# A hybrid decoder layer on one core: the split of the mixed values in four steps, and when the forgetting heads' decay rows are loaded

## Chip, core and metric

One core of one Trainium2 chip runs the whole layer in one launch. The metric is the device time of that launch in microseconds (us). Everything is float32; TensorE multiplies in a format called fp32r here, so the kernel makes a product of two or three passes over parts of its operands: the rounded value (hi) and what the rounding left (lo).

## What is computed

A layer of 1024 positions and 1024 channels: one input projection feeds eight heads with a sliding window (A) and eight forgetting heads (B), their outputs side by side go through one output projection, and an MLP follows. Of the reference:

```python
xn = rmsnorm(x, attn_norm_g)
proj = jnp.einsum('bsd,de->bse', xn, w_in)
qa, ka, va, qb, kb, vb, f_logit = jnp.split(proj, IN_SPLITS, axis=-1)
...
out_a = swa_sinks_attention(qa, ka, va, sink_logits)      # 8 heads of 64, window 128
...
log_f = jax.nn.log_sigmoid(f_logit + b_forget)
out_b = forgetting_attention(qb, kb, vb, log_f)           # 8 heads of 64, causal
mixed = jnp.concatenate([out_a, out_b], axis=-1)
x = x + jnp.einsum('bse,ed->bsd', mixed, w_out)
hn = rmsnorm(x, mlp_norm_g)
hid = jnp.square(jax.nn.relu(jnp.einsum('bsd,df->bsf', hn, w_up)))
x = x + jnp.einsum('bsf,fd->bsd', hid, w_down)
```

In a forgetting head the score of query t and key s gets c[t] - c[s] added, where c is the running sum of log f; the term c[t] falls out of the softmax, so what is left is one row of 1024 numbers a head, the **decay row**.

## The kernel before

**Stages.** The projection of the A heads and of the first pair of B heads comes first, then the A heads in two groups of eight units (`heads_a`), then the B heads in four pairs p = 0 to 3, of eight units each (`heads_b`): units 0 to 3 are the first head of the pair (h = 0), 4 to 7 the second (h = 1). A unit is 256 queries of one head, in the order `ORDER_B`. The MLP follows; it uses Strassen's scheme of seven products.

**A unit.** `scores_b` (L590) makes the score products `spb` for 128 queries and up to 512 keys at a time; VectorE adds the decay row `cb` and finds the extreme in one instruction (L607, printed as ISA), ScalarE takes the exponential. `mix_b` (L631) transposes the probabilities (`tpb`), evicts them into hi (`pth`, ScalarE, L347) and lo (`ptl`, VectorE, L348), multiplies with the values (`pvb`), joins the two accumulated parts (`mtb`, L660) and stores the result to `mix_d` in DRAM (L663; `mta`, L511, for the A heads). Scores run `DEPTH` = 2 units ahead of the mixing.

**Fillers.** Between the units stand projection products `ps` for the next pair of B heads and, in the last pair, products `po` of the output projection (`out_first`). `PACE` gives the number of units of scores behind which each is placed, and `tc.issue_after(x)` keeps an instruction behind x in the order. Their weights come as rows `wr` (L205), each into a buffer that has to be free, and are split into `wh` (cast, ScalarE) and `wl` (subtraction, POOL).

**What sets the order.** A scheduler orders each engine's instructions by modelled times and priorities; `prep` and the two offsets `HPO` and `HPA` raise the priority of what they enclose. Each engine then runs its list in order and waits where an operand or a buffer is missing. All transfers are issued by SyncE, in order too: one that waits holds up all that stand behind it.

**The mixed values.** The probabilities are not divided by their sum before the products, except in the last pair of B heads. So the 14 halves (seven pairs of heads e, two halves c of 512 positions) go back from DRAM to be divided and split, in `split_mix(e)` (L532): `mixr` is the half of `mix_d`, `mixn` the inverse sums from `rd_d`, spread over the partitions in two transfers (L538, L540); VectorE multiplies them (L541); ScalarE casts (hi) and POOL subtracts (lo); the result `mixs` is stored (L543) and loaded later as the tiles `mix0` to `mix6` for the output projection (L758). There is one buffer each of `mixr`, `mixn` and `mixs`. `SPLITS` names the unit (p, u) in which `split_mix(e)` is called; both halves are written there at once, and where they come to stand is the scheduler's choice.

**The decay rows.** `prep_k(p, h)` (L575) also loads the row `cb` of that head (L578, 512 KB, spread over 128 partitions) into one of two buffers. `ahead` calls it for h = 0 in unit 5 and for h = 1 in unit 7 of the pair before.

Of the kernel before, what the change touches and what calls it, by code (L numbers as in the profile page):

```python
# [8 lines left out]
F32 = mybir.dt.float32  # L9
# [37 lines left out]
SPLITS = ((0, 4), (0, 7), (1, 1), (1, 4), (1, 6), (2, 5), (3, 5))  # L47
# [4 lines left out]
def hybrid_layer(  # L52
# [435 lines left out]
    def mix_a(pts, g, i):  # L488
# [21 lines left out]
        for j in range(2):  # L510
            nc.sync.dma_start(mix_d[2 * g + j, :, i * P : (i + 1) * P], mt[:, j, :])  # L511
# [20 lines left out]
    def split_mix(e):  # L532

        for c in range(2):
            cs = slice(c * 512, (c + 1) * 512)
            m, q = (ap2.tile([P, 512], F32, tag=n, name=n, bufs=1) for n in ("mixr", "mixn"))
            hl = ap2.tile([P, 2, 512], F32R, tag="mixs", name="mixs", bufs=1)
            nc.sync.dma_start(m, mix_d[e][:, cs])  # L538
            for h in range(2):
                nc.sync.dma_start(q[rows_of[h], :], rd_d[2 * e + h, cs].partition_broadcast(HD))  # L540
            nc.vector.tensor_tensor(out=m, in0=m, in1=q, op=ALU.mult)  # L541
            split(hl[:, 0], hl[:, 1], m, nc.scalar, nc.gpsimd)
            nc.sync.dma_start(  # L543
                mixs_d[e][:, :, cs].rearrange("c p s -> p c s"), hl.bitcast(F32)
            )
# [29 lines left out]
    def prep_k(p, h):  # L575
        heads[p, "k1", h] = make_k_b(qkb[p], P, p, h)
        cb = ap2.tile([P, S], F32, tag="bias", name=f"cb{p}{h}", bufs=2)
        nc.sync.dma_start(cb, c_d[2 * p + h].partition_broadcast(P))  # L578
        heads[p, "cb", h] = cb
# [5 lines left out]
    def scores_b(p, qp, h):  # L585
        q1, k1, k2, cb = heads[p, "q"][h], heads[p, "k1", h], k2_of[h], heads[p, "cb", h]
        probs = []
        for i in (2 * qp, 2 * qp + 1):
# [8 lines left out]
            for c in range((nk + 511) // 512):  # L597
# [9 lines left out]
                nc.vector.tensor_tensor_reduce(  # L607
# [20 lines left out]
        marks.append(pe.ins)  # L628
        return probs

    def mix_b(probs, p, qp, h):  # L631
# [30 lines left out]
        if p < 3:  # L662
            nc.sync.dma_start(mix_d[4 + p, r, ms], mt[r, :])  # L663
        else:
            split(mh[7][r, ms], ml[7][r, ms], mt[r, :], nc.scalar, nc.vector)
# [46 lines left out]

    def heads_b(p):
        for u in range(8):
            qp, h = (ORDER_END if p == 3 and u > 3 else ORDER_B)[u % 4], u // 4
            unit(lambda: scores_b(p, qp, h), lambda got, qp=qp, h=h: mix_b(got, p, qp, h))
            if u == DEPTH:
                prep(prep_v, p, 1)
                if p:
                    prep(inverse_to, 6 + 2 * p, dn_b[(p - 1) % 2], 2)  # L720
                else:
                    prep(inverse_a)
            if (p, u) in SPLITS:
                split_mix(SPLITS.index((p, u)))
# [193 lines left out]
    def up(j):  # L918
# [3 lines left out]
        s = slot(("m5", "m4")[j % 2], "wus", [4, 4, P])  # L922
# [180 lines left out]
    def h_add(c, dt, cs):  # L1103

        nset[1] += 1
        h = slot(("m3", "m5")[nset[1] % 2], "hy", [4, 512])
# [117 lines left out]
```

## Time and profile before

| | us |
|---|---|
| device time, median of 3 runs | 1147.91 (1147.52 to 1148.44) |
| the profiled execution's own time | 1146.44 |
| its span, from the first to the last instruction | 1144.2 |
| TensorE matmul, busy | 1108.6 |
| VectorE, busy | 771.0 |
| ScalarE, busy | 576.4 |
| GpSimd, busy | 381.6 |

The mean granted clock of TensorE was 0.991. PE is TensorE's matmuls, PEld its weight loads, DVE VectorE, ACT ScalarE, POOL GpSimd, SP or SPq SyncE and its queue; L12 is line 12 of the kernel. In a row of the timeline stand the start, the duration, the engine, the line, the operation with its tiles, and in brackets how long the engine had been idle and what released it. In the busy times by stretch stand the bounds, the length, then PE, PEld, DVE, ACT and POOL with their counts of instructions, the granted clock, the share of the DMA engines and GB/s. In the groups of instructions stand the busy time and the mean ns of one, then the idle time of the engine just before them, with what ended it. The chain of work that ended last is followed back from the last instruction, at each step to what released it; "issue" is time in which the engine waited for nothing that the profile shows. In the list of waits of SyncE's queue, the engine and line after the arrow are what was waited for, then the sum, the count and the longest wait.

### The profile page before, as it was taken

What the parts mean: (1) busy time and instruction counts of PE and PEld (TensorE: products, weight loads), DVE (VectorE), ACT (ScalarE), POOL (GpSimd) and SP (SyncE); (2) the same over time, 40 slices, a digit from 0 to 9 for tenths busy, and PEclk for the clock granted to TensorE, in tenths of its full rate; (3) what the DMA queues carried; (4) which work ended last, traced back from release to release, by engine and by line L of the source; (5) the groups of instructions that cost most, each with busy time, mean ns of one, the idle gap of its engine ahead of it and who ended that gap; (6) DMA issues with size and microseconds to landing.
All of it is one profiled execution on the core that took longest, in us unless ns stands there. A gap on an engine that the chain in (4) does not pass through costs nothing.

```text
span 1144.2 us, 15605 instructions
## 1 busy us (share of the span) xinstructions
PE 1108.6 (97%) x5556; PEld 944.9 (83%) x5556; DVE 771.0 (67%) x1316; ACT 576.4 (50%) x1013; POOL 381.6 (33%) x340
## 2 busy tenths in 40 slices
PE   9999899899999999998999999999999999999998
PEld 8998799789898887786888887888888888888876
DVE  6437867756567568799767676865575876674493
ACT  5443877666567666554554544435444433333330
POOL 5651143425533645133232322322221221222241
PEclk9999999999999999999999999999999999999999
DMA  8310121244416647364455443434699777665441
GB/s 308 120 34 22 34 84 41 72 150 162 146 47 238 212 165 248 124 237 148 162 194 193 149 183 123 164 138 166 223 391 352 263 282 253 227 235 190 174 140 45
DMA packets 95646, 195.68 MB, mean 171 GB/s; under 512 B 7128, under 2 KB 19016, under 8 KB 95568
## 3 DMA queue, kind: packets, MB, share of 16 engines
q1 hardware_dynamic: 95424, 194.66, 48.5%
q8 instruction: 44, 0.72, 0.3%
q14 instruction: 34, 0.28, 0.1%
q10 hardware_dynamic: 144, 0.02, 0.0%
HBM read 141.61 MB, written 53.04 MB: 170 GB/s over the span
## 4 chain that ended last, share of the span: by engine, by line
PE 83%; DVE 8%; DMA 3%; issue 2%; ACT 2%; POOL 1%; SPq 0%; DVEq 0%; POOLq 0%; ACTq 0%
PE pd L69 26%; PE pu L69 26%; PE ps L69 12%; PE po L69 4%; PE qps L69 3%; PE spb L69 2%; PE pvb L69 2%; PE tpb L643 2%; PE sp L69 1%; PE tpa L495 1%; DVE ptl L348 1%; DMA mixr<-mix_d 1%; PE pv L69 1%; DMA h_d<-h 1%; DVE sb L607 1%
## 5 line engine op out<-in xcount | busy, mean ns | idle before, releaser
L69 PE MATMUL pd<-hx,wx 128*128 128x512 f32 x1344 | 307.1, 391 | 2.4 <-POOL wx L76 2.4
L69 PEld LDWEIGHTS pd<-hx,wx 128*128 128x128 f32 x1344 | 253.2, 189 | 56.2 <-POOL wx L76 2.9
L69 PE MATMUL pu<-bh,wu 128*128 128x512 f32 x896 | 281.4, 395 | 1.3 <-ACT bh L837 1.3
L69 PEld LDWEIGHTS pu<-bh,wu 128*128 128x128 f32 x896 | 168.7, 188 | 41.3 <-ACT bh L837 1.7
L69 PE MATMUL pu<-bl,wu 128*128 128x512 f32 x448 | 176.7, 395 | 1.9 <-DVE bl L76 1.8
L76 POOL TENSOR_TENSOR wx<-wda,wx 128x1024 fp32r<-128x1024 f32 x28 | 84.6, 3023 | 222.2 <-ACT wx L73 222.2
L73 ACT CAST hx<-hr 128x1024 fp32r<-128x1024 f32 x56 | 59.0, 1054 | 181.0 <-PE pd L69 176.1
L76 DVE TENSOR_TENSOR hx<-hr,hx 128x1024 fp32r<-128x1024 f32 x56 | 74.2, 1332 | 77.1 <-ACT hx L73 77.1
L69 PE MATMUL ps<-wh,xh 128*128 128x384 f32 (+1 forms) x320 | 111.2, 350 | 3.2 <-DVE q L193 2.5
L69 PE MATMUL ps<-wl,xh 128*128 128x384 f32 (+1 forms) x320 | 110.5, 346 | 0.7 <-POOL wl L76 0.7
L69 PE MATMUL ps<-wh,xl 128*128 128x384 f32 (+1 forms) x320 | 110.8, 347 | 0.0
L69 PEld LDWEIGHTS pu<-bl,wu 128*128 128x128 f32 x448 | 84.4, 188 | 22.6 <-DVE bl L76 2.2
L69 PE MATMUL po<-mix,wos 128*128 128x512 f32 x384 | 94.8, 396 | 1.4 <-ACT mix L73 0.8
L76 POOL TENSOR_TENSOR wu<-wus,wu 128x512 fp32r<-128x512 f32 x32 | 47.2, 1476 | 133.8 <-ACT wu L73 129.1
L69 PEld LDWEIGHTS po<-mix,wos 128*128 128x128 f32 x384 | 70.5, 188 | 16.4 <-ACT mix L73 1.5
L73 ACT CAST wu<-wus 128x512 fp32r<-128x512 f32 x64 | 39.1, 618 | 82.6 <-PE pu L69 75.9
L76 POOL TENSOR_TENSOR wu<-wur,wu 128x512 fp32r<-128x512 f32 x32 | 44.0, 1377 | 88.9 <-ACT wu L73 88.9
L76 POOL TENSOR_TENSOR wl<-wr,wh 128x384 fp32r<-128x384 f32 (+1 forms) x47 | 50.0, 1075 | 54.4 <-ACT wh L73 42.2
L905 DVE TENSOR_TENSOR ht<-hb 128x512 f32<-128x512 f32 x32 | 21.8, 722 | 67.1 <-ACT hb L960 67.1
L348 DVE TENSOR_TENSOR ptl<-tpb,pth 128x512 fp32r<-128x512 f32 (+1 forms) x80 | 50.0, 633 | 22.1 <-ACT pth L347 21.5
L69 PEld LDWEIGHTS ps<-wh,xh 128*128 128x128 f32 x320 | 61.3, 192 | 4.2 <-issue 2.8
L69 PEld LDWEIGHTS ps<-wl,xh 128*128 128x128 f32 x320 | 61.3, 192 | 1.9 <-POOL wl L76 1.3
(213 smaller groups left out, 2068.4 us busy)
## 6 DMA issues: line engine op xcount, KB each, us to landing
wda<-in_w_d_dram SPq DMA_DIRECT2D x34, 1024.0 KB, 8.5
hr<-hid_d SPq DMA_DIRECT2D x56, 512.0 KB, 6.2
wur<-in_w_u_dram SPq DMA_DIRECT2D x32, 512.0 KB, 3.6
hid_d<-ht SPq DMA_DIRECT2D x16, 1024.0 KB, 4.4
hid_d<-hb SPq DMA_DIRECT2D x16, 768.0 KB, 3.6
mixs_d<-mixs SPq DMA_DIRECT2D x14, 512.0 KB, 3.4
mix<-mixs_d SPq DMA_DIRECT2D x7, 1024.0 KB, 8.9
wr<-in_w_b_dram SPq DMA_DIRECT2D x32, 192.0 KB, 2.6
```

Of the source, the lines that this page charges most:

```text
L69: return nc.tensor.matmul(out, lhsT, rhs, start=start, stop=stop)
L73: hi_eng.copy(hi, src)
L76: lo_eng.tensor_tensor(out=lo, in0=src, in1=hi.bitcast(F32), op=ALU.subtract)
L348: nc.vector.tensor_tensor(out=lo[:, cols], in0=pt[:, cols], in1=hi[:, cols].bitcast(F32), op=ALU.subtract)
L495: nc.tensor.transpose(tp[:, hh * P : (hh + 1) * P], pts[hh // 2][:, hh % 2, c0 : c0 + P], ident)
L607: nc.vector.tensor_tensor_reduce(out=pr[:, c * 512 : c * 512 + n], in0=sp[:, :n], in1=cb[:, c * 512 : c * 512 + n], scale=1.0, scalar=3e38 ...
L643: nc.tensor.transpose(tp[:, c0 : c0 + P], probs[qi][:, kb * P : (kb + 1) * P], ident)
L905: eng.tensor_tensor(out=out, in0=a, in1=b, op=ALU.subtract)
```

## The change

`split_mix` no longer issues anything itself. It returns four steps: load half 0; multiply and split half 0, load half 1; store half 0, multiply and split half 1; store half 1. `heads_b` runs one of them in each unit, the first in the unit that `SPLITS` names, and six of its seven entries are earlier than before by one or two units. All loads and stores of these steps are kept behind the latest store of mixed values (`stored`), and the products behind the latest reduction of scores (`reduced`). `mixs` has two buffers instead of one.

The decay row of a pair's first head is still asked for in `prep_k`, but behind the latest store of mixed values. That of the second head is asked for in unit 1 of its own pair (`load_c`), not in unit 7 of the pair before.

In the MLP two groups of buffers, `wus` for even j and half of `hy`, move from the pool `zl` on the left side of the memory to `zr` on the right side, under the tag `m5`.

```diff
-SPLITS = ((0, 4), (0, 7), (1, 1), (1, 4), (1, 6), (2, 5), (3, 5))
+SPLITS = ((0, 4), (0, 6), (1, 0), (1, 2), (1, 4), (2, 4), (3, 3))
...
+            st = nc.sync.dma_start(mix_d[2 * g + j, :, i * P : (i + 1) * P], mt[:, j, :])
+        stored.append(st.ins)
...
     def split_mix(e):
...
-            hl = ap2.tile([P, 2, 512], F32R, tag="mixs", name="mixs", bufs=1)
-            nc.sync.dma_start(m, mix_d[e][:, cs])
+            behind(m, mix_d[e][:, cs])
             for h in range(2):
-                nc.sync.dma_start(q[rows_of[h], :], rd_d[2 * e + h, cs].partition_broadcast(HD))
-            nc.vector.tensor_tensor(out=m, in0=m, in1=q, op=ALU.mult)
+                behind(q[rows_of[h], :], rd_d[2 * e + h, cs].partition_broadcast(HD))
+
+        def make(c):
+            m, q = got[c]
+            hl = got[c] = ap2.tile([P, 2, 512], F32R, tag="mixs", name="mixs", bufs=2)
+            with tc.issue_after(reduced[-1]):
+                nc.vector.tensor_tensor(out=m, in0=m, in1=q, op=ALU.mult)
             split(hl[:, 0], hl[:, 1], m, nc.scalar, nc.gpsimd)
-            nc.sync.dma_start(
-                mixs_d[e][:, :, cs].rearrange("c p s -> p c s"), hl.bitcast(F32)
-            )
+
+        def store(c):
+            cs = slice(c * 512, (c + 1) * 512)
+            behind(mixs_d[e][:, :, cs].rearrange("c p s -> p c s"), got[c].bitcast(F32))
+
+        return [
+            lambda: load(0),
+            lambda: (make(0), load(1)),
+            lambda: (store(0), make(1)),
+            lambda: store(1),
+        ]
+
+    stored, reduced = [], []
+
+    def behind(out, in_):
+        with tc.issue_after(stored[-1]):
+            nc.sync.dma_start(out, in_)
...
     def prep_k(p, h):
         heads[p, "k1", h] = make_k_b(qkb[p], P, p, h)
-        cb = ap2.tile([P, S], F32, tag="bias", name=f"cb{p}{h}", bufs=2)
-        nc.sync.dma_start(cb, c_d[2 * p + h].partition_broadcast(P))
-        heads[p, "cb", h] = cb
+        if h == 0:
+            load_c(p, 0)
+
+    def load_c(p, h):
+        cb = heads[p, "cb", h] = ap2.tile([P, S], F32, tag="bias", name=f"cb{p}{h}", bufs=2)
+        behind(cb, c_d[2 * p + h].partition_broadcast(P))
...
-                nc.vector.tensor_tensor_reduce(
+                ttr = nc.vector.tensor_tensor_reduce(
...
+        reduced.append(ttr.ins)
...
-            nc.sync.dma_start(mix_d[4 + p, r, ms], mt[r, :])
+            stored.append(nc.sync.dma_start(mix_d[4 + p, r, ms], mt[r, :]).ins)
...
+            if u == 1:
+                load_c(p, 1)
+            for step in [st.pop(0) for st in splitting if st]:
+                step()
             if (p, u) in SPLITS:
-                split_mix(SPLITS.index((p, u)))
+                splitting.append(split_mix(SPLITS.index((p, u))))
+                splitting[-1].pop(0)()
...
-        s = slot(("m5", "m4")[j % 2], "wus", [4, 4, P])
+        s = slot(*(("m4", "wus", [4, 4, P]), ("m5", "wus", [4, 4, P], F32, "zr"))[j % 2 == 0])
...
-        h = slot(("m3", "m5")[nset[1] % 2], "hy", [4, 512])
+        h = slot(*(("m3", "hy", [4, 512]), ("m5", "hy", [4, 512], F32, "zr"))[nset[1] % 2])
```

How the order of the engines changes is shown at three places. The number behind a name counts tiles and differs between the two kernels.

VectorE in the first pair of B heads, from one `mtb` on (mixed values of one unit, first row) over the products of the split (`mixr`) to the next evictions `ptl`; `q1b` are queries of the next pair, `ss` a reduction for their norm. Before:

```order
L660 TENSOR_TENSOR mtb_2754<-pvb_2724,tmpb_2752 64x256
L541 TENSOR_TENSOR mixr_3108<-mixr_3108,mixn_3109 128x512
L275 SCALAR_TENSOR_TENSOR q1b10_2777<-ptq_2788,gqk_72,q1b10_2777 64x512
L275 SCALAR_TENSOR_TENSOR q1b11_2778<-ptq_2788,gqk_72,q1b11_2778 64x512
L348 TENSOR_TENSOR ptl_2856<-tpb_2850,pth_2855 128x512
L235 TENSOR_REDUCE ss_2955<-sq_2953 128x16
L541 TENSOR_TENSOR mixr_3118<-mixr_3118,mixn_3119 128x512
L240 SCALAR_TENSOR_TENSOR ss_2955<-ss_2955,ep2_77 128x16
L348 TENSOR_TENSOR ptl_2869<-tpb_2863,pth_2868 128x512
```

And with the change, from the same `mtb` on:

```order
L689 TENSOR_TENSOR mtb_2754<-pvb_2724,tmpb_2752 64x256
L635 ISA sb_2972,nmb_2973<-spb_2975,cb01_2481 128x512
L635 ISA nmb_2973 128x1
L275 SCALAR_TENSOR_TENSOR q1b11_2763<-ptq_2773,gqk_72,q1b11_2763 64x512
L348 TENSOR_TENSOR ptl_2841<-tpb_2835,pth_2840 128x512
L551 TENSOR_TENSOR mixr_2757<-mixr_2757,mixn_2758 128x512
L235 TENSOR_REDUCE ss_2949<-sq_2947 128x16
L348 TENSOR_TENSOR ptl_2854<-tpb_2848,pth_2853 128x512
```

Of the two products between this `mtb` and the second `ptl` one is left, and it stands behind the first `ptl` and ahead of the reduction; a score reduction (L635) of the second head has come up.

SyncE's queue later in the same pair, where weight rows `wr` of the next projection and pieces of the split are issued, before:

```order
L543 DMA mixs_d_82<-mixs_3347 128x2x512
L538 DMA mixr_3667<-mix_d_81 128x512
L540 DMA mixn_3678<-rd_d_87 64x512 x2
L663 DMA mix_d_81<-mtb_3105 64x256
L205 DMA wr_3461<-in_w_b_dram 128x384
L205 DMA wr_3467<-in_w_b_dram 128x384
L205 DMA wr_3473<-in_w_b_dram 128x384
L543 DMA mixs_d_82<-mixs_3669 128x2x512
L538 DMA mixr_3677<-mix_d_81 128x512
L205 DMA wr_3479<-in_w_b_dram 128x384
```

And with the change:

```order
L570 DMA mixr_3006<-mix_d_81 128x512
L570 DMA mixn_3007<-rd_d_87 64x512
L205 DMA wr_3465<-in_w_b_dram 128x384
L692 DMA mix_d_81<-mtb_3109 64x256
L570 DMA mixs_d_82<-mixs_3002 128x2x512
L570 DMA mixn_3118<-rd_d_87 64x512 x2
L205 DMA wr_3471<-in_w_b_dram 128x384
L570 DMA mixr_3117<-mix_d_81 128x512
L205 DMA wr_3477<-in_w_b_dram 128x384
L205 DMA wr_3483<-in_w_b_dram 128x384
```

The weight row that stood behind a pair of `mixn` loads and a store of mixed values (`wr_3461`, now `wr_3465`) stands ahead of them; the rows behind it stand between and behind the next piece's loads.

VectorE in the third pair of B heads (p = 2), at the first score reductions of its second head, which read the row `cb21`. Before:

```order
L660 TENSOR_TENSOR mtb_4242<-pvb_4186,tmpb_4240 64x256
L607 ISA sb_4462,nmb_4463<-spb_4465,cb21_4055 128x128
L607 ISA nmb_4463 128x1
L348 TENSOR_TENSOR ptl_4384<-tpb_4378,pth_4383 128x512
L348 TENSOR_TENSOR ptl_4397<-tpb_4391,pth_4396 128x512
L607 ISA sb_4471,nmb_4472<-spb_4474,cb21_4055 128x256
```

And with the change; the load of `cb21` is issued right behind the store of the `mtb` in the first row, where before it was issued a pair earlier:

```order
L689 TENSOR_TENSOR mtb_4240<-pvb_4184,tmpb_4238 64x256
L348 TENSOR_TENSOR ptl_4384<-tpb_4378,pth_4383 128x512
L348 TENSOR_TENSOR ptl_4397<-tpb_4391,pth_4396 128x512
L348 TENSOR_TENSOR ptl_4409<-tpb_4404,pth_4408 128x384
L348 TENSOR_TENSOR ptl_4487<-tpb_4481,pth_4486 128x512
L348 TENSOR_TENSOR ptl_4499<-tpb_4494,pth_4498 128x384
L275 SCALAR_TENSOR_TENSOR q1b30_4518<-ptq_4520,gqk_72,q1b30_4518 64x512
L689 TENSOR_TENSOR mtb_4340<-pvb_4323,tmpb_4338 64x256
L275 SCALAR_TENSOR_TENSOR q1b31_4519<-ptq_4520,gqk_72,q1b31_4519 64x512
L635 ISA sb_4462,nmb_4463<-spb_4465,cb21_4243 128x128
```

The first reduction stood right behind that `mtb` and now stands behind five `ptl`, two `q1b` and the next `mtb`; the second head's score products stand later on TensorE accordingly.

More of the change, by code (lines that the diff above doesn't have):

```diff
@@ L510, in mix_a @@
         for j in range(2):
-            nc.sync.dma_start(mix_d[2 * g + j, :, i * P : (i + 1) * P], mt[:, j, :])
+            st = nc.sync.dma_start(mix_d[2 * g + j, :, i * P : (i + 1) * P], mt[:, j, :])
+        stored.append(st.ins)
     def inverse_to(first, dn, n):
@@ L711, in heads_a @@
             fill()
+    splitting = []
     def heads_b(p):
```

7 lines of the change are left out of this document (5 added, 2 removed).

## The prediction

> **What bounds the kernel now.** I read the page first, then the busy times by stretch, then the chain that ended last, then the rows of each engine where TensorE stood still.
>
> ```profile
> span 1144.2 us, 15605 instructions
> PE 1108.6 (97%) x5556; PEld 944.9 (83%) x5556; DVE 771.0 (67%) x1316; ACT 576.4 (50%) x1013; POOL 381.6 (33%) x340
> PE 83%; DVE 8%; DMA 3%; issue 2%; ACT 2%; POOL 1%; SPq 0%; DVEq 0%; POOLq 0%; ACTq 0%
> ```
>
> TensorE is busy for 97% of the span, so an edit outside it can only give back what TensorE loses by waiting. Where that is, the stretches show (length, then PE busy first):
>
> ```profile
> 200.00:229.00 29.00, 26.05 (x146) 21.40 (x145) 21.41 (x54) 19.77 (x44) 12.72 (x14) 0.94 0.26 73
> 241.00:258.00 17.00, 14.52 (x94) 13.57 (x92) 10.60 (x21) 10.41 (x22) 5.03 (x4) 0.97 0.42 133
> 281.00:298.00 17.00, 14.54 (x92) 12.26 (x91) 11.24 (x25) 9.75 (x24) 13.29 (x18) 1.00 0.53 170
> 298.00:352.00 54.00, 53.76 (x358) 50.70 (x357) 31.88 (x80) 33.34 (x72) 14.94 (x24) 1.00 0.21 65
> 352.00:372.00 20.00, 18.46 (x127) 15.41 (x126) 18.05 (x49) 15.72 (x37) 9.39 (x15) 1.00 0.89 338
> 372.00:424.00 52.00, 51.98 (x295) 44.19 (x294) 27.61 (x66) 32.97 (x68) 27.69 (x30) 1.00 0.58 191
> 424.00:456.00 32.00, 30.50 (x187) 25.46 (x186) 27.47 (x70) 22.07 (x49) 18.09 (x25) 1.00 0.66 227
> 528.00:1144.20 616.20, 609.14 (x2640) 497.26 (x2640) 413.56 (x480) 251.23 (x283) 166.68 (x87) 1.00 0.56 201
> ```
>
> From 528 us the MLP runs, which the diff touches only in the place of two buffers. The forgetting heads run from 200 to 456. There TensorE is idle 2.95 in the first stretch, 2.48 in 241:258, 2.46 in 281:298, 0.24, 1.54, 0.02 and 1.50 in the rest. The two 17 us stretches are those in which the mixed values are split; the chain goes through them:
>
> ```profile
> 244.20 4.24 DMA mixr<-mix_d
> 248.56 0.70 DVE mixr L541
> 249.28 0.63 ACT mixs L73
> 249.98 1.30 POOL mixs L76
> 251.30 0.38 SPq L543
> 251.72 4.03 DMA mixr<-mix_d
> 255.94 0.69 DVE mixr L541
> 256.71 0.61 DVE ptl L348
> ```
>
> One piece of the split follows the other through load, product, cast, subtraction and store, some 7.4 us from load to load, and its product stands in VectorE's queue ahead of `ptl`, for which the value products wait.
>
> **First stall, 241:258.** The rows of VectorE, and TensorE's wait behind them:
>
> ```profile
> 246.89 0.42 DVE L660 TENSOR_TENSOR mtb<-pvb,tmpb 64x256 f32<-64x256 f32 x1
> 253.16 1.22 DVE L235 TENSOR_REDUCE ss<-sq 128x16 f32<-128x1024 f32 x1 [0.66 <-POOL sq L230]
> 255.94 0.69 DVE L541 TENSOR_TENSOR mixr<-mixr,mixn 128x512 f32<-128x512 f32 x1 [1.55 <-DMA mixr<-mix_d]
> 256.63 0.68 DVE L348 TENSOR_TENSOR ptl<-tpb,pth 128x512 fp32r<-128x512 f32 x1
> ```
> ```profile
> 257.37 0.58 PE L69 MATMUL pvb<-ptl,vb 128*128 128x256 f32 x1 [2.48 <-DVE ptl L348]
> ```
>
> The product waits 1.55 for its load and takes 0.69, together 2.24 ahead of that `ptl`. The change has one product in this place, and it comes earlier: behind the first `ptl` and ahead of the reduction `ss`. When its load lands I work out from the issue times and these landings:
>
> ```profile
> cb<-c_d SPq DMA_DIRECT2D x8, 512.0 KB, 3.8
> mixr<-mix_d SPq DMA_DIRECT2D x14, 256.0 KB, 4.0
> mixn<-rd_d SPq DMA_DIRECT2D x28, 128.0 KB, 3.0
> ```
>
> `mtb` ends at 247.3. Its store and the load of `mixr` take about 0.5 each to issue, so `mixr` is issued at 247.8 and lands at 251.8, the second `mixn` at about 252. The product ends near 252.7, before POOL's `sq` releases the reduction at 253.16. So the product lies in a wait that is there anyway, and the `ptl` ends 2.2 us earlier. **Term: -2.2** (bounds -2.48, all the idle time, and 0, if the load lands after 254.4 and the product stands ahead of `ss` for as long as now). The load's wait itself does not vanish; it is moved to where something else waits too.
>
> [...]
>
> **Second stall, 281:298.** SyncE's queue, then POOL and ScalarE:
>
> ```profile
> 275.21 0.47 SPq L538 DMA_DIRECT2D mixr<-mix_d  x1
> 281.22 1.09 SPq L540 DMA_DIRECT2D mixn<-rd_d  x2
> 282.42 0.53 SPq L663 DMA_DIRECT2D mix_d<-mtb  x1
> 283.00 1.60 SPq L205 DMA_DIRECT2D wr<-in_w_b_dram  x3
> ```
> ```profile
> 279.64 1.01 POOL L76 TENSOR_TENSOR wl<-wr,wh 128x384 fp32r<-128x384 f32 x1 [4.59 <-ACT wh L73]
> ```
> ```profile
> 286.40 0.51 ACT L73 CAST wh<-wr 128x384 fp32r<-128x384 f32 x1 [3.68 <-DMA wr<-in_w_b_dram]
> ```
>
> The fourth weight row of the last projection needs the buffer that POOL frees at 280.65. It goes out at 283.00, since the `mixn` pair ahead of it waits for the product that frees `mixn`. It reaches ScalarE 3.40 later, and ScalarE, with the `pth` casts behind the weight's, stands for 3.68. In the changed queue this row is ahead of that pair and of the store: it can go out at about 280.7 and arrive at 284.1, 2.3 earlier. ScalarE's wait falls to about 1.4. The later rows do not gain as much: rows six to eight now stand behind a `mixr` load that waits for POOL's subtraction (now 283.00 + 1.28 = 284.28), where rows five and six go out at 283 to 284.6 now. **Term: -2.0** of the 2.46 idle (bounds -2.46 and 0).
>
> **The other pieces.** Nothing is added to the work: the 14 products, 14 `mixr` and 28 `mixn` loads, 14 `mixs` stores and 8 `cb` loads stay, in another order. The second `mixs` buffer gets no credit, since the chain goes from the store's issue to the next load and not to a cast; nor do the two buffers of the MLP that move to the other side, since they are as large and as many as now. The products:
>
> ```profile
> L541 DVE TENSOR_TENSOR mixr<-mixr,mixn 128x512 f32<-128x512 f32 x14 | 11.9, 852 | 12.7 <-DMA mixr<-mix_d 5.4 <-POOL ptl L649 3.5 <-issue 2.6
> ```
>
> VectorE stood 12.7 us ahead of them, and I expect about as much again, since the new order puts most of them two to six VectorE instructions behind the store that their load follows. Six fall into 298:352, where two fall now and TensorE is idle for 0.24 of 54 us: projection products cover them. Cost 0 (up to 1.5 if that cover ends early). The last pair, 424:456, comes out as it is: about the same products ahead of it, 0 (bounds -1.5 and +1).
>
> **The decay rows.** They are what may cost. A second head's row was loaded a pair ahead, and its load blocked SyncE:
>
> ```profile
> SPq L578 <- DVE nmb L607: 18.8, 5, 10.5
> ```
>
> Behind the longest, 10.5 us, stood only stores, so I credit nothing for it. Now each row follows the store of the pair before, about 0.9 of issues later, and lands 3.8 after that (3.6 to 7.4):
>
> ```profile
> DMA to landing us min/median/max: 3.6/3.8/7.4
> ```
>
> That is about 4.7 behind the `mtb` named in the order. What VectorE has to do meanwhile:
>
> ```profile
> L348 DVE TENSOR_TENSOR ptl<-tpb,pth 128x512 fp32r<-128x512 f32 x48 | 32.6, 687 | 16.3 <-ACT pth L347 16.0
> L348 DVE TENSOR_TENSOR ptl<-tpb,pth 128x384 fp32r<-128x384 f32 x32 | 17.6, 551 | 5.9 <-ACT pth L347 5.5
> L660 DVE TENSOR_TENSOR mtb<-pvb,tmpb 64x256 f32<-64x256 f32 x32 | 13.3, 415 | 11.1 <-ACT tmpb L658 10.5
> L275 DVE SCALAR_TENSOR_TENSOR q1b<-ptq,gqk,q1b 64x512 fp32r<-64x512 f32 x12 | 9.0, 749 | 4.4 <-ACT q1b L274 4.2
> ```
>
> Pair 2: three and two `ptl` (2.06 and 1.10), one `mtb` (0.42), two `q1b` (1.50), 5.1 in all: no wait at 3.8, some 3.2 at 7.4. The transfers there run at 338 GB/s (stretch 352:372), so it may well be late. Worse, five groups of score products that TensorE had there move behind the first output products, which wait for their own weights. 13 matmuls at some 0.2 are 2.6 at most; TensorE then has 24 output products to go on with. I take **+0.8** (0 to +3.2). Pair 1: a reduction, an `mtb` and a `ptl`, 1.8 to 1.9 of VectorE work, against 4.7, a wait of 2.8; TensorE has 22 projection products in front, 3.3 at the 0.15 that one took in 298:352: 0 (up to +2.8). Pairs 0 and 3: 2.5 and 3.6 of work, with 24 projection and 13 output products to cover: 0. The very first row, `cb00`, now follows a late store of the window heads, so three score reductions move behind three `ptl` in 200:229, where TensorE has no filler. They cover 128, 256 and 512 columns, an estimated 1.4 together at the 0.69 that a `ptl` of 512 takes. VectorE's idle time there takes up half: **+0.7** (0 to +1.9, with 0.5 of waiting for the row itself).
>
> **Sum.** -2.2 - 2.0 + 0.8 + 0.7 = -2.7 us. The profiled execution took 1146.44 (span 1144.2 and 2.24 around it), 1.47 below the median of the runs shown; it would become 1143.7. I put the difference on the median, 1147.91, and predict **1145.2**. A measurement of this kernel can tell 0.2% from no change, 2.3 us, so this is just faster.
>
> **Rivals.**
> - All three idle times of the split go (2.48 + 2.46 + 1.50 = 6.4) and the rows cost nothing: 1141.5. For it: the chain's own rows. Against: the products still wait for loads of 4.0 us. Chance 0.17.
> - The change doesn't do what it says: with one `mixr` and one `mixn` buffer the second load of a pair still waits for POOL, so pieces go in series as now, weights six to eight are held behind `mixr`, and half of the first term and all of the second are lost: -1.1 + 1.5 = +0.4, 1148.3. For it: the 12.7 us above stay in the order. Against: the fourth row's place in SyncE's queue. Chance 0.28.
> - Slower: VectorE, in order, stands at the first score reduction of a second head until its row lands. From the point at which TensorE's fillers are shorter than that wait, it is exposed: at `cb00`, pair 1 and pair 2 together 1.9 + 2.8 + 3.2 = 7.9, less 4.2: +3.7, 1151.6. For it: the landings of up to 7.4 and the moved score products. Against: TensorE idle for only 0.24 us in 298:352. Chance 0.17.
> - My forecast, 1142.8 to 1147: 0.38.
>
> Two thirds of the forecast (0.25), all of the first rival and 0.05 of the second lie over 0.2% below 1147.91: faster 0.47. Slower: 0.17, and 0.02 of the second rival: 0.19. The rest, 0.34, is no change. The range, 1140.9 to 1150.6, leaves out about half of the first and of the third rival.
>
> **What would show it.** Right: in the changed profile no wait of 2 us before `pvb` where the first product stands; ScalarE's longest wait before `wh` under 2; TensorE idle under 1 in each stretch that answers to 241:258 and 281:298; VectorE's idle before the products still near 10. Wrong: `wh` still waiting 3 us or more; a score reduction that waits over 2 us for `cb` with TensorE idle beside it; TensorE idle over 3 us more around the first output products.

## The result, and the profile after

The changed kernel takes **1160.26 us** (median of 5 runs, 1158.46 to 1162.37), the kernel before 1147.52 in the same comparison (5 runs, 1141.36 to 1148.44). The ratio is **1.0125**, with a 95% interval of 1.0098 to 1.0152: slower by some 14 us, where 1145.2 was predicted and the range ended at 1150.6. From here on "slower by" is this ratio less one, against runs of the kernel before on the same chip.

The page of the changed kernel: its span, the busy times and the shares of the chain that ended last.

```profile
span 1158.0 us, 15593 instructions
PE 1114.4 (96%) x5556; PEld 945.1 (82%) x5556; DVE 774.4 (67%) x1316; ACT 576.8 (50%) x1013; POOL 382.7 (33%) x340
PE 76%; DVE 9%; DMA 7%; issue 3%; ACT 2%; POOL 1%; SPq 1%; DVEq 0%; POOLq 0%; ACTq 0%
```

TensorE's work is the same 5556 products, but the chain now runs through DMA for 7% of the span (3% before) and through TensorE for 76% (83%). The busy times by stretch say where. The stretches are cut at the first score product of the forgetting heads, the first output product and the first product of the MLP; first the kernel before, then the changed one (bounds, length, PE busy, then the other engines, granted clock, DMA share, GB/s).

```profile
0.00:201.40 201.40, 189.14 (x1100) 179.41 (x1101) 127.54 (x338) 119.42 (x301) 83.36 (x89) 0.97 0.29 92
201.40:369.90 168.50, 158.84 (x1016) 143.74 (x1014) 111.26 (x272) 110.10 (x242) 65.53 (x92) 0.98 0.40 135
369.90:512.20 142.30, 138.74 (x752) 115.08 (x752) 104.43 (x213) 86.94 (x174) 59.76 (x69) 1.00 0.58 196
512.20:1144.20 632.00, 621.92 (x2693) 506.63 (x2691) 427.81 (x495) 259.92 (x298) 172.99 (x91) 1.00 0.55 200
```
```profile
0.00:197.40 197.40, 186.89 (x1100) 177.06 (x1101) 128.48 (x338) 119.89 (x302) 83.41 (x89) 0.99 0.27 88
197.40:372.70 175.30, 159.73 (x1004) 141.78 (x1002) 109.49 (x262) 108.06 (x237) 64.71 (x91) 0.98 0.41 132
372.70:526.10 153.40, 145.64 (x762) 119.81 (x763) 107.94 (x223) 88.43 (x179) 59.32 (x69) 0.97 0.56 188
526.10:1158.00 631.90, 622.09 (x2693) 506.44 (x2691) 428.51 (x495) 260.44 (x298) 175.24 (x91) 1.00 0.55 200
```

The MLP is the same (632.0 and 631.9). The first stretch is 4.0 shorter, with the clock at 0.99 for 0.97; it differs as much between profiles of the same order (197.5 in the kernel with only the buffers moved, below), so it is no effect of the change. All the loss is in the forgetting heads: 168.5 becomes 175.3 and 142.3 becomes 153.4, **17.9 us** together. TensorE's idle time there (length less PE busy) grows from 13.2 to 23.3; the clock loses 8.5 us for 3.4 (each 2 us slice by one less its granted clock); the rest, some 3, is spread.

**Where TensorE stands.** SyncE's queue, VectorE and TensorE of the changed kernel around the first row of the last pair (start, duration; in brackets the idle time before and what ended it):

```profile
398.58 0.47 SPq L692 DMA_DIRECT2D mix_d<-mtb  x1
399.10 0.58 SPq L570 DMA_DIRECT2D cb<-c_d  x1
399.72 0.49 SPq L570 DMA_DIRECT2D mixr<-mix_d  x1
400.25 1.09 SPq L570 DMA_DIRECT2D mixn<-rd_d  x2
```
```profile
401.26 0.56 DVE L348 TENSOR_TENSOR ptl<-tpb,pth 128x384 fp32r<-128x384 f32 x1
406.06 0.29 DVE L635 CUSTOM_DVE_ANT_0 sb<-spb,cb 128x128 f32<-128x128 f32 x1 [4.24 <-DMA cb<-c_d]
...
407.58 0.69 DVE L551 TENSOR_TENSOR mixr<-mixr,mixn 128x512 f32<-128x512 f32 x1 [0.87 <-DMA mixn<-rd_d]
408.19 0.68 DVE L348 TENSOR_TENSOR ptl<-tpb,pth 128x512 fp32r<-128x512 f32 x1
```
```profile
403.06 0.60 PE L672 MATMUL tpb<-ident,sb 128*128 128x128 f32 x4
406.42 0.80 PE L69 MATMUL spb<-k1b,q1b 128*128 128x512 f32 x1 [2.76 <-DVE nmb L635]
```

The row goes out right behind a store, at 399.10, and lands 6.8 later, with the split's loads beside it. VectorE comes to the reduction that reads it at 401.8 and stands for 4.24; TensorE runs out of other work at 403.66 and stands for 2.76, since its next output products are behind the next score product in its queue.

The other large stall, in the second pair, has a product of the split in it; VectorE, then TensorE:

```profile
324.37 0.17 DVE L240 SCALAR_TENSOR_TENSOR ss<-ss,ep 128x16 f32<-128x16 f32 x1
326.97 0.69 DVE L551 TENSOR_TENSOR mixr<-mixr,mixn 128x512 f32<-128x512 f32 x1 [2.42 <-DMA mixn<-rd_d]
...
327.78 0.69 DVE L348 TENSOR_TENSOR ptl<-tpb,pth 128x512 fp32r<-128x512 f32 x1
```
```profile
325.57 0.39 PE L69 MATMUL pvb<-pth,vb 128*128 128x256 f32 x1 [1.73 <-ACT pth L347]
328.52 0.58 PE L69 MATMUL pvb<-ptl,vb 128*128 128x256 f32 x1 [2.57 <-DVE ptl L348]
```

The first wait, 1.73, is ScalarE's, which stood for a reduction of the norm; the second, 2.57, is the product's, which stands in VectorE for 2.42 ahead of the `ptl`.

This stall cost more than its length. The same place in slices of 2 us; the third number from the right is the granted clock:

```profile
326.00:328.00 2.00, 0.00 (x0) 0.00 (x0) 1.00 (x3) 0.26 (x1) 0.00 (x0) 0.95 0.02 8
328.00:330.00 2.00, 1.48 (x7) 1.48 (x8) 1.75 (x5) 0.36 (x1) 1.57 (x4) 0.50 0.00 0
330.00:332.00 2.00, 2.00 (x11) 1.85 (x10) 1.76 (x5) 1.19 (x3) 2.00 (x4) 0.50 0.00 0
332.00:334.00 2.00, 2.00 (x9) 1.54 (x9) 1.04 (x5) 1.74 (x4) 1.45 (x4) 0.50 0.04 8
334.00:336.00 2.00, 2.00 (x12) 1.68 (x11) 1.54 (x5) 1.40 (x4) 1.01 (x1) 0.84 0.00 0
```

TensorE is back at work at 328.52, at half clock until about 334.6: 0.1 + 1.0 + 1.0 + 1.0 + 0.3 = 3.4 us, of which some 0.4 fall into the wait itself and 3.0 come on top of it. By group, over both stretches, VectorE's idle time (third number) ahead of the products and of the smallest reductions, the first of a head:

```profile
L551 DVE TENSOR_TENSOR mixr<-mixr,mixn 128x512 f32<-128x512 f32 x14 | 10.5, 750 | 22.0 <-DMA mixn<-rd_d 18.3 <-DMA mixr<-mix_d 3.6
L635 DVE CUSTOM_DVE_ANT_0 sb<-spb,cb 128x128 f32<-128x128 f32 x8 | 2.3, 292 | 14.8 <-DMA cb<-c_d 14.1 <-PE spb L69 0.7
```

Products: 22.0, where it was 12.7 (17.4 in e3 below, which has the order of the kernel before). Rows: 14.1 here and 2.8 at the last pair's second head, 16.9 in all, where it was nothing.

### The profile page after: what moved, and what is told of

The parts are those of the page before. It is cut to its first block, busy times and chain, and to the rows that moved or that the text cites. A ratio compares the mean times of both kernels' runs of the same rounds, so it can differ in the third digit from the quotient of the medians.

```text
span 1158.0 us, 15593 instructions
## 1 busy us (share of the span) xinstructions
PE 1114.4 (96%) x5556; PEld 945.1 (82%) x5556; DVE 774.4 (67%) x1316; ACT 576.8 (50%) x1013; POOL 382.7 (33%) x340
## 4 chain that ended last, share of the span: by engine, by line
PE 76%; DVE 9%; DMA 7%; issue 3%; ACT 2%; POOL 1%; SPq 1%; DVEq 0%; POOLq 0%; ACTq 0%
PE pu L69 26%; PE pd L69 26%; PE ps L69 10%; PE po L69 4%; PE pvb L69 2%; PE spb L69 2%; DMA mixn<-rd_d 2%; PE tpb L672 2%; PE sp L69 1%; DMA cb<-c_d 1%; PE pv L69 1%; PE tpa L495 1%; DVE ptl L348 1%; DMA xq<-in_x_dram 1%; DMA xr<-in_xT_dram 1%
## 5 line engine op out<-in xcount | busy, mean ns | idle before, releaser
L348 DVE TENSOR_TENSOR ptl<-tpb,pth 128x512 fp32r<-128x512 f32 (+1 forms) x80 | 50.3, 633 | 25.8 <-ACT pth L347 25.1
L641 ACT ACTIVATE sb<-sb,nmb 128x128 f32<-128x128 f32 (+3 forms) x64 | 49.7, 777 | 33.1 <-DVE nmb L635 32.8
```

What stands on the lines that cost most here:

```text
L348: nc.vector.tensor_tensor(out=lo[:, cols], in0=pt[:, cols], in1=hi[:, cols].bitcast(F32), op=ALU.subtract)
L641: nc.scalar.activation(pr[:, :nk], pr[:, :nk], AF.Exp, scale=-1.0, bias=nm[:, c : c + 1], accum_out=dn_b[p % 2][:, h, i : i + 1] if p < 3 ...
```

## The experiments

All thirteen, with one profile each. The stretches are those above (first score to first output product, and from there to the MLP); "idle" is TensorE's in both, "clock" the time lost to it there, "rows" and "products" VectorE's idle time behind either, all in us.

| kernel | split | rows | slower by (95%) | stretches | idle | clock | rows | products |
|---|---|---|---|---|---|---|---|---|
| before | at once | early | 0 | 168.5, 142.3 | 13.2 | 3.4 | 0 | 12.7 |
| changed | four steps | late | 1.25% (0.98 to 1.52) | 175.3, 153.4 | 23.3 | 8.5 | 16.9 | 22.0 |
| e1 | four steps | early | -0.04% (-0.21 to 0.12) | 169.5, 143.0 | 15.1 | 3.4 | 0 | 20.6 |
| e2 | at once | late | 0.66% (0.47 to 0.84) | 168.6, 152.4 | 19.3 | 5.1 | 18.7 | 15.7 |
| e3 | at once | early | -0.06% (-0.23 to 0.11) | 170.8, 142.6 | 15.4 | 3.4 | 0 | 17.4 |
| e4 | four steps | first heads' late | 0.53% (0.38 to 0.69) | 177.5, 142.5 | 20.3 | 6.8 | 7.8 | 25.1 |
| e11 | four steps | second heads' late | 0.65% (0.41 to 0.89) | 170.5, 149.2 | 20.4 | 5.1 | 6.8 | 22.4 |
| e6 | four steps | a unit earlier | 1.48% (1.09 to 1.87) | 176.2, 151.2 | 25.0 | 8.5 | 1.4 | 27.3 |
| e10 | at once | a unit earlier | 0.37% (0.16 to 0.57) | 170.2, 149.8 | 20.7 | 1.7 | 1.4 | 29.2 |
| e13 | four steps | early, scores held | 0.69% (0.44 to 0.94) | 170.9, 150.1 | 19.4 | 6.8 | 0 | 30.1 |
| e14 | at once | early, scores held | 0.01% (-0.19 to 0.21) | 170.0, 146.7 | 16.9 | 5.1 | 0 | 19.7 |
| e7 | at once | early, three buffers | -0.08% (-0.27 to 0.11) | 169.4, 144.0 | 14.9 | 3.4 | 0 | 18.9 |
| e8 | later products | early | -0.06% (-0.29 to 0.18) | 169.9, 144.8 | 18.5 | 1.7 | 0 | 21.1 |
| e9 | later products | late | 1.19% (0.87 to 1.51) | 176.0, 153.9 | 26.6 | 8.5 | 13.0 | 24.6 |
| e12 | loads free | early | 0.41% (0.18 to 0.64) | 173.0, 148.4 | 19.1 | 8.5 | 0 | 23.1 |

### Rows or split: e1 to e4 and e11

**e1**, the changed kernel with the rows as before:

```diff
-        if h == 0:
-            load_c(p, 0)
-    def load_c(p, h):
         cb = heads[p, "cb", h] = ap2.tile([P, S], F32, tag="bias", name=f"cb{p}{h}", bufs=2)
-        behind(cb, c_d[2 * p + h].partition_broadcast(P))
+        nc.sync.dma_start(cb, c_d[2 * p + h].partition_broadcast(P))
...
-            if u == 1:
-                load_c(p, 1)
```

> The changed kernel, but both heads' decay rows are asked for a pair ahead as before, and not behind a store. Theory R (the late rows cost most of the time): the three waits of VectorE of 2.5, 4.2 and 2.8 us for a row go, with them some 6 us of TensorE's idle time and two stretches of half clock at 1.7 each; about 1151 (1149 to 1153). Theory S (the products of the split, which stand ahead of the evictions until their loads land, cost most): the wait of TensorE of 4.6 us at 323 to 328 and its half clock stay; about 1157 (1155 to 1159). Theory M (the two moved buffers of the MLP): 1160, no change.

No difference from before is left, a gain larger than either theory's. So the loss needs the rows; the split in four steps alone gives nothing and costs nothing. What moves the rows is the edge alone: with `behind` replaced by a plain transfer and the rows asked for where the change does (unit 1 of the pair for the second head), all five engines are given the same instructions in the same order as in e1; that kernel was only built, not run.

**e2**, the other way round: `split_mix`, its call and `SPLITS` as before, the rows as changed.

> The changed kernel, but the mixed values are split as before (both halves at once, the units of before, one buffer of the split result); the decay rows stay as changed. Theory R: most of the loss stays; 1155 to 1158, and VectorE waits again over 2 us for a row at the first reductions of the last pair; since no mixed values are loaded right behind the row, the row lands after about 3.9 and not 5 to 7. Theory S: 1149 to 1152, and VectorE's idle time ahead of the 14 products falls from 22.0 to about 13. Theory M: 1160.

Half of the loss stays (0.66%), so neither part has all of it: rows 0.66, split -0.04, both 1.25. The expected 3.9 for a row's landing was wrong. It was 5.1, although the split's loads stand right behind the row in only three of eight places, against 5.4 in the changed kernel and 3.8 in e1. The landings in e1, e2 and the changed kernel, in this order (median us from issue to landing):

```profile
cb<-c_d SPq DMA_DIRECT2D x7, 512.0 KB, 3.8
```
```profile
cb<-c_d SPq DMA_DIRECT2D x8, 512.0 KB, 5.1
```
```profile
cb<-c_d SPq DMA_DIRECT2D x8, 512.0 KB, 5.4
```

**e3**, the kernel before with the two MLP buffers on the other side:

```diff
-        s = slot(("m5", "m4")[j % 2], "wus", [4, 4, P])
+        s = slot(*(("m4", "wus", [4, 4, P]), ("m5", "wus", [4, 4, P], F32, "zr"))[j % 2 == 0])
...
-        h = slot(("m3", "m5")[nset[1] % 2], "hy", [4, 512])
+        h = slot(*(("m3", "hy", [4, 512]), ("m5", "hy", [4, 512], F32, "zr"))[nset[1] % 2])
```

> The kernel before with nothing but the two groups of MLP buffers moved to the right side. Theories R and S: as before, 1147.5 within 0.2% (the MLP took 627.0 us before and 626.7 after). Theory M: 1155 or more.

Nothing, as expected. Its order is that of the kernel before, so the two lines of the table also show what one profile is worth: 2.6 us over the two stretches, and 4.7 us in VectorE's wait for products.

**e4**, the second head's row a pair ahead again, but still behind a store:

```diff
-        if h == 0:
-            load_c(p, 0)
+        load_c(p, h)
...
-            if u == 1:
-                load_c(p, 1)
```

> The changed kernel, but the second head's row is asked for in unit 7 of the pair before, still behind the latest store; the first head's row stays as changed. Theory R: the waits for the rows of second heads go (2.5 in the second pair, 2.8 in the last), the wait of 4.2 for the last pair's first row stays with TensorE idle for 2.9 and half clock behind it; about 1155 (1153 to 1157). If the half clock is only a mark of the stall and no cost of its own, the gain is what TensorE's idle time there was, 2.4, so 1158. Theory S: 1160.

The size fits theory R (0.53%, some 6 us), the place doesn't: the last pair's first row still made VectorE wait, 2.5 us, with no idle time of TensorE beside it. The stretch after the first output product is as before (142.5); the loss is in the one ahead of it, with one stall of 4.60 behind a weight's cast and one of 4.52 behind a product of the split. The first of them on TensorE:

```profile
288.11 0.69 PE L69 MATMUL ps<-wh,xh 128*128 128x384 f32 x1 [4.60 <-ACT wh L73]
```

**e11**, the complement, the first heads' rows without the edge:

```diff
-        behind(cb, c_d[2 * p + h].partition_broadcast(P))
+        if h == 0:
+            nc.sync.dma_start(cb, c_d[2 * p + h].partition_broadcast(P))
+        else:
+            behind(cb, c_d[2 * p + h].partition_broadcast(P))
```

> The changed kernel with the first heads' rows loaded without an edge behind a store; the second heads' rows as changed. If the two kinds of row add up (1.25% for both, 0.53% measured for the first heads' alone): 0.7%, 1154 to 1155, with the stretch from the first score to the first output product at 166 to 170 us (169.5 with both rows early) and that from there to the MLP at 150 to 154. If the last pair's first row makes the loss of the last stretch (TensorE idle for 2.8 us behind it): 143 to 148 there, and 1148 to 1150 in all.

The two kinds add up: 0.53 and 0.65, together 1.18, measured 1.25. (In e4 the second heads' rows are early but still behind a store, so its 0.53 is not the first heads' rows with all else as in e1.) And they cost in different places: the first heads' rows ahead of the first output product (e4), the second heads' mostly behind it (149.2, where 150 to 154 was expected).

### Lateness or order: e6, e10, e13 and e14

**e6** asks for both rows a unit earlier, still behind the latest store (unit 0 for unit 1, unit 4 of the pair before for unit 5). The first heads' rows are then asked for outside `prep_k`, and so also lose the raised priority that `prep` gave them.

> The changed kernel, both heads' rows still behind the latest store, but asked for one unit earlier (second head in unit 0 of its pair, first head in unit 4 of the pair before). On VectorE 5 to 16 large instructions now stand between that store's operand and the first reduction that reads the row; in the changed kernel 1 to 8. At 0.4 to 0.7 us each, with the idle time between them, that is 5 to 15 us, where a row took 5.4 to land. Theory R (the rows are late, and nothing else about them costs): VectorE waits under 3 us in all for rows (16.9 in the changed kernel), and the time falls to that of the run with early rows, 1146 to 1149. Rival B (the bunch of transfers right behind each store costs, not its lateness): 1154 or more, since the bunches stay.

The waits for rows went (1.4 for 16.9), the time did not: theory R as it stood falls. VectorE waits for products instead, 27.3. One piece of the split, the same in e1 and e6, shows how a wait of one kind becomes a stall or does not. VectorE and TensorE of e1:

```profile
402.45 0.69 DVE L551 TENSOR_TENSOR mixr<-mixr,mixn 128x512 f32<-128x512 f32 x1 [2.96 <-DMA mixn<-rd_d]
```
```profile
398.19 3.89 PE L69 MATMUL po<-mix,wos 128*128 128x512 f32 x16
401.92 0.39 PE L69 MATMUL spb<-k1b,q1b 128*128 128x512 f32 x1
```

and of e6:

```profile
409.33 0.69 DVE L551 TENSOR_TENSOR mixr<-mixr,mixn 128x512 f32<-128x512 f32 x1 [4.20 <-DMA mixn<-rd_d]
409.94 0.55 DVE L348 TENSOR_TENSOR ptl<-tpb,pth 128x384 fp32r<-128x384 f32 x1
```
```profile
410.55 0.39 PE L69 MATMUL pvb<-ptl,vb 128*128 128x256 f32 x1 [3.66 <-DVE ptl L348]
```

In e1 TensorE has 16 output products in front and no gap; in e6, where 13 score products have moved and the output products with them, it stands for 3.66.

**e10** is e6's place of the rows with the split as before.

> The split as before, the rows behind the latest store but asked for a unit earlier than in the changed kernel. Theory L (late rows alone cost): rows in time, products as before, so 1146 to 1149. Theory O (a row tied to a store changes the order: the scheduler holds the score products that read it back, here too 13 of the third pair's from ahead of the first output product to behind it, and the waits that stay stand where TensorE has less in front of it): the stretch from the first output product to the MLP, 142.2 us before and 152.4 with the split as before and the rows as changed, stays over 148; total 1151 to 1156.

0.37%: of the 0.66 on this split some is left without row waits, and the last stretch is over 148, as theory O said; 1150.94 is just below its range. VectorE's wait for products is 29.2. Three of the rows stand close ahead of the split's loads in SyncE's queue here too.

**e13** and **e14** part the two. The rows are early, nothing waits for them, but the reductions that read them are held behind the mixed values of a unit (e13 on the split in four steps, e14 on the split as before):

```diff
+            if u == 2 and joined:
+                held[p, 1] = joined[-1]
+            if u == 6 and p < 3:
+                held[p + 1, 0] = joined[-1]
...
-                ttr = nc.vector.tensor_tensor_reduce(
+                with tc.issue_after(held[p, h]) if (p, h) in held else nullcontext():
+                    ttr = nc.vector.tensor_tensor_reduce(
```

`joined` lists the `mtb` instructions. In both, 166 score products stand ahead of the first output product, as in the changed kernel and e6, and not 179 as before.

> The run with early rows and the split in four steps, but the score reductions of each head are ordered behind mixed values of one unit later than those whose store the changed kernel's row follows. So the rows are early and no one waits for them, while the order is held back much as in the changed kernel (the same 13 score products stand behind the first output product, and the output products of the last pair are spread as there). Theory L (waiting for the late rows costs): 1146 to 1148. Theory O (the held order costs: later waits fall where TensorE has less in front of it): 1153 to 1160, with the stretch from the first output product to the MLP at 148 us or more and the whole stretch of the forgetting heads, half clock taken off, at 316 or more (309.1 with early rows and free order, 320.2 in the changed kernel).

> The same order edge on the score reductions with early rows, on the split as before. Theory L: 1146 to 1147.5, and the stretch from the first output product to the MLP at 142 plus 3 us for the 13 moved products. Theory O: 1150 to 1156, like the rows a unit earlier on this split (0.37%) or the rows as changed (0.66%).

On the split as before the held order costs nothing (0.01%; its 146.7 has the moved products in it, some 3 of which the first stretch is rid), so there the loss of e2, 0.66%, comes with the rows behind a store, not with the held order. VectorE stands 18.7 us for them in e2; but e10, with 1.4 us of such waits, still loses 0.37%, so how much of the 0.66 is this standing, and how much the place of the rows' transfers, is not shown. On the split in four steps the held order alone costs 0.69%, though no row is late, and the late rows bring it to 1.25%. The interplay that was missing between e1, e2 and the changed kernel is this: four steps alone, nothing; held order alone, nothing; both, 0.69. Theory O named the mechanism, its expected 316 us for the stretches without the clock's loss was too high (314.2). VectorE's rows of e13:

```profile
L551 DVE TENSOR_TENSOR mixr<-mixr,mixn 128x512 f32<-128x512 f32 x14 | 9.7, 690 | 30.1 <-DMA mixn<-rd_d 22.8 <-DMA mixr<-mix_d 7.2
L632 DVE CUSTOM_DVE_ANT_0 sb<-spb,cb 128x128 f32<-128x128 f32 x8 | 2.3, 287 | 0.3
```

### Attempts at a faster kernel: e7, e8, e9, e12

**e7** is the kernel before with three buffers of rows (`bufs=3` on the tag `bias`, and e3's edit for the room).

> The kernel before with three buffers of decay rows in place of two (and the two MLP buffers on the right side, which frees the room). SyncE waited 18.8 us in all for a row's buffer before. If those waits of SyncE held up mixed values that TensorE needed: 1143 to 1145. If only stores stood behind the longest, as the prediction said: no change, 1146.5 within 0.2%.

No change in the time, but the edit did not take the waits away: SyncE still waits 15.5 us, at most 10.3, behind the reductions (18.8 and 10.5 before). So e7 does not tell what these waits cost.

**e8** (on e1) and **e9** (on the changed kernel) put the products later:

```diff
             lambda: load(0),
-            lambda: (make(0), load(1)),
+            lambda: load(1),
+            lambda: make(0),
             lambda: (store(0), make(1)),
             lambda: store(1),
...
-                ap2.tile([P, 512], F32, tag=n, name=n, bufs=1) for n in ("mixr", "mixn")
+                ap2.tile([P, 512], F32, tag=n, name=n, bufs=2) for n in ("mixr", "mixn")
```

(and one buffer of `mixs`).

> The run with early rows, and the product of half 0 one unit later than its load, that of half 1 two (two buffers each of the loads, one of the result). Theory S (in that run the products' waits for their loads, 20.6 us on VectorE, are what eats the gain; two stalls of TensorE of 2.6 and 2.7 us and a half clock stand behind them): VectorE's idle time before the products falls under 6, the two stalls go, and the time to 1141 to 1144. If the waits only move to other instructions: 1146 within 0.2%.

> The changed kernel with the products one unit later in the same way; the rows stay as changed. Theory R: the loss of the late rows stays; 1153 to 1156, like the run with the rows alone. If rows and products cost only together (a late row holds VectorE, and a product's wait comes on top), 1147 to 1150.

The edit did not do what was meant: VectorE stands 21.1 and 24.6 ahead of the products, against 20.6 and 22.0 without the edit. The part of this that a load ended did fall, to 13.5 in e8 (19.4 in e1) and 12.0 in e9 (21.9), but other waits took its place. So e8 and e9 can't decide on theory S, which asked for under 6 in all; e9 repeats the changed kernel's loss.

**e12** (on e1) loads the split's operands without the edge, into two buffers each:

```diff
-                ap2.tile([P, 512], F32, tag=n, name=n, bufs=1) for n in ("mixr", "mixn")
+                ap2.tile([P, 512], F32, tag=n, name=n, bufs=2) for n in ("mixr", "mixn")
...
-            behind(m, mix_d[e][:, cs])
+            nc.sync.dma_start(m, mix_d[e][:, cs])
...
-                behind(q[rows_of[h], :], rd_d[2 * e + h, cs].partition_broadcast(HD))
+                nc.sync.dma_start(q[rows_of[h], :], rd_d[2 * e + h, cs].partition_broadcast(HD))
```

> The run with early rows, and the loads of mixed values and inverse sums without the edge behind a store, into two buffers each (one of the result): they go out as soon as a buffer is free. Theory S (the loads' place behind a store makes the products wait, 20.6 us on VectorE there, and hides what the four steps give): VectorE waits under 12 us for products, TensorE's idle time from the first score to the MLP falls from 15.1 to 11 or less, 1141 to 1144. If the stalls only move: 1146 within 0.2%.

Slower by 0.41%, and 23.1 us of waits for products: a miss. No kernel tried beats the one before by more than the measurement can tell.

## Why the prediction was wrong

Two steps failed. The rows were priced at +0.8 and +0.7; against e1, which lacks only their edge, they cost 1.29% (1.25 and 0.04), some 15 us. And the four steps, priced at -2.2 and -2.0, gave nothing that can be told from no change (e1).

**First stall, -2.2,** and **second, -2.0.** Of the changed kernel, VectorE's first product, and ScalarE's longest wait for that group of weights:

```profile
247.25 0.69 DVE L551 TENSOR_TENSOR mixr<-mixr,mixn 128x512 f32<-128x512 f32 x1 [1.51 <-DMA mixn<-rd_d]
```
```profile
278.23 0.51 ACT L73 CAST wh<-wr 128x384 fp32r<-128x384 f32 x1 [1.30 <-DMA wr<-in_w_b_dram]
```

The first stall went: from 236 to 253 TensorE is idle 0.4 us, where it was 2.48. The reason was in part another one than given. `sq` was done at 246.05, ahead of the product, so the product held the reduction `ss` back and did not lie in a wait for `sq`; TensorE had other work. The second term was mis-sized: the cast waits 1.30, predicted about 1.4, but TensorE is idle 1.8 us from 272 to 289, and 2.2 in e1 from 280 to 297, where it was 2.46. A stall of 1.3 or 1.4 stands there now behind a product that waits for its load. And what was gained is gone elsewhere: e1, which has both terms and no late row, is as fast as before, with TensorE idle for 15.1 us over the two stretches (13.2 before, 15.4 in e3).

"VectorE stood 12.7 us ahead of them, and I expect about as much again" failed too: it is 20.6 in e1 and 22.0 in the changed kernel. With 17.4 in e3 one profile can't tell all of that from chance; the part that a load ended is clearer, 6.4 and 11.2 in the order before (the kernel before, e3), 19.4 and 21.9 in e1 and the changed kernel. A stall of some 2.6 stands in both in the second pair, at a piece that the sum had at 0, behind "projection products cover them": in the changed kernel the product holds `ptl`, in e1 its cast holds ScalarE's `pth`. TensorE's row of e1:

```profile
328.50 0.39 PE L69 MATMUL pvb<-pth,vb 128*128 128x256 f32 x1 [2.56 <-ACT pth L347]
```

That a mean of 0.24 idle in 54 us shows cover was true of the old order only. The other points:

- **The rows, +0.8 and +0.7: the step that decided.** "Pairs 0 and 3 ... to cover: 0" was said of the second heads, and there is no term at all for the first heads' rows of pairs 1 to 3, though the diff ties these to a store too. Measured apart on the split in four steps, the first heads' rows cost 0.53% and the second heads' 0.65%, some 6 and 7.5 us. The largest single stall of TensorE is behind the last pair's first row; the prediction had named such a one, "over 2 us for `cb` with TensorE idle beside it", as a sign of being wrong. For `cb00`, which got the +0.7, VectorE did not wait.
- **The landing.** 3.8 was taken, from rows of which only one of eight went out right behind a store; in the changed kernel it was 5.4 in the median and up to 6.8. With one or two large instructions on VectorE between that store's operand and the reduction, as for the first rows of pairs 1 and 2, even 3.8 would have been too long.
- **Moved score products.** 13 moved, as said. That this moves the output products between them too, and so takes away what TensorE had in front when a product waits, was not seen; with the four steps it makes 0.69%.
- **The clock.** A granted clock of 0.94 and 0.97 stands in the rows that the prediction quotes, and no term was made of it. In the two stretches it makes 5.1 of the 17.9 us.
- **What cost nothing** as said: the two MLP buffers (e3). Whether SyncE's waits for the rows' buffers cost nothing, as said too, stays open (e7).
- **The rivals.** The slower one had the mechanism, "VectorE, in order, stands at the first score reduction ... until its row lands", but named pair 1, pair 2 and `cb00`, missed the last pair, and gave 1151.6 and a chance of 0.17.

Still open: why e6, where rows are in time and as many score products are moved as in e13, is slower than e13 (1.48% and 0.69%). In e6 four of the rows stand right behind a store of mixed values and 0.6 to 1.4 us ahead of the split's loads in SyncE's queue; in e13 these stand ahead of that store, 1.5 to 2.2 us before the loads. That this is the difference was argued, not tried, nor was the lost priority. The same question is open for e10 and e14 on the split as before (0.37% and 0.01%). Nor is e13's order the changed kernel's in every place, so its 0.69% is the cost of an order of that kind, not exactly of that one.

## What to carry to other kernels

An order edge on a load is an order edge on everything that reads it (13 score products moved with the rows here): before tying a prefetch to a store, count for every reader what its engine has to do between that store's operand and the read, and compare it with the landing behind a store (5.4 us in the median in the changed kernel), not with the landing alone (3.8 in e1). Whether a wait of VectorE stalled TensorE hung on what stood in front of TensorE at that place (2.96 in e1, behind 16 output products, left no gap; 4.20 in e6 left TensorE idle for 3.66), and an edit that moves fillers moves this cover; an idle share of nearly zero in the old order does not vouch for the new one. Price a long stall of TensorE with the half clock that may come with it, 1.7 or 3.4 us more in the changed kernel's trace, and take that loss off before two single profiles are compared.

## What the runs showed of the hardware

In the forgetting heads of the changed kernel TensorE ran at a granted clock of 0.50 three times: for 6.83 us from 327.81, behind stalls of 1.73 and 2.57 close together; for 3.41 from 406.32, at the end of one of 2.76; and for 6.83 from 450.69, at the end of one of 1.39 with two of 0.3 beside it. So each lost up to 1.7 or 3.4 us more. The losses per stretch in the table come in such steps (1.7, 3.4, 5.1, 6.8, 8.5). The three begin 78.51 and 44.37 us apart, 23 and 13 times 3.41.

Not every stall brought this: in e13 TensorE was idle for 2.97 of the 4 us from 326.27, in e14 for 3.00 of the 6 us from 251.96, and the granted clock stayed at 1.00. Nor did the time at work just ahead settle it: in the 3.41 us before each of the eleven half clocks in the traces of the kernel before and of the changed one (that at the end of the changed one's span left out) TensorE was busy for 0.39 to 2.05 us, before the three above for 0.39, 0.74 and 1.84; in the changed kernel's MLP it was busy for 1.76 of the 3.41 from 1129.95, with a stall of 2.43 in it, and the clock stayed at 1.00. So the clock's part of a loss can't be read from the length of a stall alone; what else it hangs on was not shown. From run to run of one kernel, too, the time goes with the clock: of the 18 runs of the kernel before beside e13, the shortest span was 1139.5 at a mean granted clock of 0.997, the longest 1150.6 at 0.988.

The same load of a row took 0.32 to 0.38 to issue in the kernel before and 0.42 to 0.59 behind a store in the changed one, but for one of 0.34 where SyncE had paused for 1.36 ahead of it. No run tells why.
